# A 128-byte copy per DMA engine as ScalarE's first act, in a rotary-embedding kernel

## Chip, cores, metric

One core of a Trainium2 chip. The metric is device time in microseconds (us); medians are of three to eleven runs, and come with their range or with the ratio to the kernel before and its 95% interval.

## The reference

```python
batch, seq, dim = 16, 512, 1024      # 16 heads of 64, float32
x1, x2 = x[..., :32], x[..., 32:]    # per head
out = concat([x1 * cos - x2 * sin, x1 * sin + x2 * cos], axis=-1)
```

`cos` and `sin` are 512 x 32 and are shared by all batches and heads. `x` and `out` have 33.55 MB each.

## The kernel before

Each of the 16 batches is one tile of 128 partitions x 16 KB (2048 KB). SyncE issues all loads, ScalarE all stores; ten tiles fit into SBUF, so loads 10 to 15 wait for the store of the tile ten before. Between load and store GpSimd and VectorE multiply, and VectorE or TensorE with ScalarE add.

```python
def on_sync(sp):
    for c in range(NC):                               # 16 tiles
        if c * R >= RING:                             # from the 11th: buffer must be free
            sp.wait_ge(sem_out[c - RING // R], 16)
        sp.dma_start(tile(c), xv[c]).then_inc(sem_in[c], 16)
        if c == 0:
            ...                                       # cos and sin to SBUF, 64 KB each
    sp.wait_ge(sem_rest, 16 * (NC - len(sem_out)))

def on_scalar(ae):
    ae.wait_ge(sem_sin, 16)
    sv = ...
    ae.activation(s_sb[:, :, 0, :], sv, COPY, scale=-1.0)
    ae.activation(s_sb[:, :, 1, :], sv, COPY).then_inc(sem_s, 1)
    for u in range(NU):                               # 64 units, 4 a tile
        ...                                           # empties PSUM for some of them
        if r == R - 1:
            wait_added(ae, u)
            ae.dma_start(ov[c], tile(c)).then_inc(...)    # store of tile c
```

## Time and profile before

| | before |
|---|---|
| time, median of the 3 runs before the prediction | 161.97 us (161.94 to 162.54) |
| span of the profiled run | 160.5 us |
| DMA engines full | 38 of 40 slices |
| first load issued, first store issued | 0.80 us, 22.09 us |

Three lines of the timeline (start, duration, engine; ACTq and SPq are DMA issues of ScalarE and SyncE):

```profile
0.80 1.28 ACT L135 ACT_TABLE_LOAD   x1 [0.80 <-PEq L268]
0.80 0.37 SPq L124 DMA_DIRECT2D x_sb<-in_x_dram  x1
...
22.09 0.38 ACTq L144 DMA_DIRECT2D out_dram<-x_sb  x1
```

ScalarE and SyncE start together at 0.80 us. ScalarE's queue has nothing to issue before that first store at 22.09 us.

### The profile page before, as it was taken

The page shows a single profiled execution, that of the slowest core. Times are in us where ns is not written, and L with a number is a line of the kernel's source. Part 1 is how long each engine was busy: PE and PEld are TensorE (multiplying, and loading weights), DVE is VectorE, ACT ScalarE, POOL GpSimd, SP SyncE. Part 2 cuts the span into 40 slices and gives each one's busy share as a digit, 9 for nine tenths or more (in the row PEclk, how much of TensorE's full clock was granted, in tenths as well). Part 3 has the DMA queues.
Part 4 walks back from the last instruction along what each step waited for, and adds up shares of the span by engine and source line. Part 5 has one row for each costly group of instructions (what it writes and reads, how often), then busy time and mean ns, then how long its engine had stood idle before and what let it go on. Part 6 is the DMA issues. An engine that isn't in the chain of part 4 may idle for free.

```text
span 160.5 us, 607 instructions
## 1 busy us (share of the span) xinstructions
PE 81.7 (51%) x102; PEld 25.4 (16%) x102; DVE 131.5 (82%) x116; ACT 26.3 (16%) x27; POOL 130.3 (81%) x62
## 2 busy tenths in 40 slices
PE   6004928354833944854573584575485436576000
PEld 1002402110210220211022021122022002112000
DVE  0089299999999879999999699998999799969400
ACT  3010221122022022012202202211211220220200
POOL 1069999999999999999999993998939988498000
PEclk9999996879595558595765555765567795567555
DMA  5999999999999999999999999999999999999996
GB/s 151 404 445 429 433 429 404 412 441 421 433 445 416 441 433 418 441 421 437 431 425 441 421 441 425 433 437 420 441 429 429 433 425 441 429 429 437 421 435 290
DMA packets 4899, 67.27 MB, mean 419 GB/s; under 512 B 544, under 2 KB 800, under 8 KB 800
## 3 DMA queue, kind: packets, MB, share of 16 engines
q1 hardware_dynamic: 2592, 33.69, 49.9%
q10 hardware_dynamic: 2304, 33.56, 48.8%
q14 instruction: 3, 0.02, 0.0%
HBM read 33.69 MB, written 33.55 MB: 419 GB/s over the span
## 4 chain that ended last, share of the span: by engine, by line
DVE 36%; PE 19%; issue 17%; POOL 10%; ACT 5%; DMA 5%; SPq 0%; DVEq 0%; POOLq 0%
PE t_ps L164 19%; DVE x_sb L235 18%; DVE t_ps L224 15%; POOL t_sb L193 10%; ACT x_sb L141 5%; DMA stage<-in_sin_dram 5%; DVE t_sb L215 4%; SPq L127 0%; SPq L124 0%; ACT s_sb L135 0%; ACT s_sb L136 0%; DVEq L234 0%; DVEq L223 0%; POOLq L116 0%; DVEq L221 0%
## 5 line engine op out<-in xcount | busy, mean ns | idle before, releaser
L193 POOL TENSOR_TENSOR t_sb<-x_sb,s_sb 128x1024 f32<-128x1024 f32 x56 | 129.6, 2376 | 17.0 <-DMA x_sb<-in_x_dram 8.9
L164 PE MATMUL t_ps<-t_sb,ident 128*128 128x512 f32 x96 | 78.9, 972 | 65.8 <-DVE t_ps L224 49.8
L224 DVE TENSOR_TENSOR t_ps<-x_sb,tab_ps 128x1024 f32<-128x1024 f32 x64 | 77.1, 1227 | 10.4 <-ACT x_sb L141 8.6
L235 DVE TENSOR_TENSOR x_sb<-t_ps,t_sb 128x1024 f32<-128x1024 f32 x40 | 48.6, 1217 | 0.0
L141 ACT ACTIVATE x_sb<-t_ps 128x1024 f32<-128x1024 f32 x24 | 24.6, 1023 | 115.8 <-PE t_ps L164 100.9
L164 PEld LDWEIGHTS t_ps<-t_sb,ident 128*128 128x128 f32 x96 | 24.7, 281 | 119.4 <-DVE t_ps L224 86.4
L215 DVE TENSOR_TENSOR t_sb<-x_sb,tab_ps 128x1024 f32<-128x1024 f32 x8 | 9.7, 1210 | 0.0
L202 DVE COPY tab_ps<-stage 128x128 f32<-128x128 f32 x1 | 0.3, 294 | 7.6 <-DMA stage<-in_cos_dram 7.6
L150 PE MATMUL t_ps<-zero 128*128 128x512 bf16 x6 | 2.7, 630 | 1.3 <-DVE zero L198 1.3
L135 ACT ACTIVATE s_sb<-stage 128x128 f32<-128x128 f32 x1 | 0.3, 309 | 6.9 <-DMA stage<-in_sin_dram 6.9
L135 ACT ACT_TABLE_LOAD x1 | 1.3, 1283 | 0.8 <-PEq L268 0.8
L150 PEld LDWEIGHTS t_ps<-zero 128*128 128x128 bf16 x6 | 0.7, 137 | 2.4 <-DVE zero L198 1.2
L198 DVE MEMSET zero<- 128x256 uint32 x1 | 0.3, 272 | 0.9 <-PEq L268 0.9
L175 POOL MEMSET ident<- 128x128 f32 x1 | 0.2, 204 | 0.3 <-POOLq L268 0.3
L177 POOL TENSOR_SCALAR_AFFINE_SELECT ident<-ident 128x128 f32<-128x128 f32 x1 | 0.3, 292 | 0.1
L268 POOL MEMSET const-float32-0.0<- 128x1 f32 x1 | 0.1, 98 | 0.3 <-issue 0.3
L136 ACT ACTIVATE s_sb<-stage 128x128 f32<-128x128 f32 x1 | 0.3, 293 | 0.0
L204 DVE TENSOR_SCALAR tab_ps<-stage 128x128 f32<-128x128 f32 x1 | 0.3, 283 | 0.0
L205 DVE COPY tab_ps<-stage 128x128 f32<-128x128 f32 x1 | 0.3, 283 | 0.0
L268 POOL MEMSET const-bfloat16-1.0<- 128x1 bf16 x1 | 0.1, 101 | 0.0
L268 POOL MEMSET const-uint8-127<- 128x1 uint8 x1 | 0.1, 101 | 0.0
L268 POOL MEMSET const-float32-1.0<- 128x1 f32 x1 | 0.1, 98 | 0.0
## 6 DMA issues: line engine op xcount, KB each, us to landing
x_sb<-in_x_dram SPq DMA_DIRECT2D x16, 2048.0 KB, 52.5
out_dram<-x_sb ACTq DMA_DIRECT2D x16, 2048.0 KB, 19.3
stage<-in_cos_dram SPq DMA_DIRECT2D x1, 64.0 KB, 7.5
stage<-in_sin_dram SPq DMA_DIRECT2D x1, 64.0 KB, 7.2
```

Of the source, the lines that this page charges most:

```text
L135: ae.activation(s_sb[:, :, 0, :], sv, COPY, scale=-1.0)
L136: ae.activation(s_sb[:, :, 1, :], sv, COPY).then_inc(sem_s, 1)
L141: ae.activation(xs[:, k, :], t1_ps[:, u % NT1, :], COPY).then_inc(sem_a, 1)
L150: pe.matmul(t1_ps[:, k, b * BANK:(b + 1) * BANK], zero[:, 0:P], zero[:], start=True, stop=True).then_inc(sem_w, 1)
L164: ins = pe.matmul(t1_ps[:, u % NT1, b * BANK:(b + 1) * BANK], ident[:], t2[:, b * BANK:(b + 1) * BANK], start=False, stop=True, skip_group ...
L177: pl.affine_select(out=ident[:], in_=ident[:], compare_op=mybir.AluOpType.is_equal, fill=0.0, base=0, pattern=[[-1, P]], channel_multiplier=1,
L193: pl.tensor_tensor(t2_sb[:, u % NT2, :, :, :], swapped(k), sin_of(s_sb, r), mult).then_inc(sem_p, 1)
L198: ve.memset(zero[:], 0.0).then_inc(sem_z, 1)
L215: ve.tensor_tensor(t2_sb[:, u % NT2, :, :, :], swapped(k), sin_of(s_ps, r), mult).then_inc(sem_d, 1)
L224: ve.tensor_tensor(t1_ps[:, u % NT1, :].rearrange("p (h d) -> p h d", d=HALF), x_sb[:, k, :, :, :].rearrange("p h t d -> p (h t) d"), c_ps ...
L235: ve.tensor_tensor(xs[:, k, :], t1_ps[:, u % NT1, :], t2_sb[:, u % NT2, :, :, :].rearrange("p h t d -> p (h t d)"), add,).then_inc(sem_v, 1)
L268: nc = _bacc.Bacc("TRN2", target_bir_lowering=False, num_devices=1)
```

## The change

Its intent, as I read it, is that every DMA engine makes one small copy as its first act: 128 bytes from HBM to HBM, into a row of `out`. Whatever an engine's first write there costs would then be paid before the first store, which overwrites the row. The store waits for the copy, so the order is safe. In what follows the copy is called the touch.

```diff
+        sem_touch = stack.enter_context(nc.semaphore("touch"))
 ...
         def on_scalar(ae):
+            ae.dma_start(out[0, 0:seq:seq // 16, 0, 0:HALF], cos[0:seq:seq // 16, :]).then_inc(sem_touch, 16)
             ae.wait_ge(sem_sin, 16)
 ...
                 if r == R - 1:
+                    if c == 0:
+                        ae.wait_ge(sem_touch, 16)
                     wait_added(ae, u)
```

## The prediction

> **What bounds the kernel now.** I read the busy shares first, then the DMA row, then the waits of the loading queue, then the first and last microseconds.
>
> ```profile
> span 160.5 us, 607 instructions
> PE 81.7 (51%) x102; PEld 25.4 (16%) x102; DVE 131.5 (82%) x116; ACT 26.3 (16%) x27; POOL 130.3 (81%) x62
> DMA  5999999999999999999999999999999999999996
> GB/s 151 404 445 429 433 429 404 412 441 421 433 445 416 441 433 418 441 421 437 431 425 441 421 441 425 433 437 420 441 429 429 433 425 441 429 429 437 421 435 290
> ...
> q1 hardware_dynamic: 2592, 33.69, 49.9%
> q10 hardware_dynamic: 2304, 33.56, 48.8%
> ...
> HBM read 33.69 MB, written 33.55 MB: 419 GB/s over the span
> ```
>
> No compute engine is above 82%, but the 16 DMA engines are full in 38 of the 40 slices. 67.1 MB must move (16 loads and 16 stores of 2048 KB each), and the flat part of the GB/s row lies near 430. 67.1 MB / 430 GB/s is 156 us of the 160.5. The other 4.5 us are the start, the end and a few slow places. The chain of waits names VectorE and TensorE, but it follows semaphores and cannot see a queue that is never empty. The waits of the loading queue say it plainly:
>
> ```profile
> SPq L124 <- DMA out_dram<-x_sb: 76.1, 6, 29.1
> SPq L130 <- DMA out_dram<-x_sb: 74.0, 1, 74.0
> ```
>
> Six loads wait 76.1 us in total for an earlier store to leave its buffer; then the queue waits 74.0 us for the last stores. So an engine-microsecond of DMA counts wherever it is spent between the first packet and the last, and nothing else does. To see what time the change could touch I cut the span into stretches (columns: stretch, its length, busy time of each compute engine, TensorE clock, DMA share, GB/s):
>
> ```profile
> 0.00:0.50 0.50, 0.00 (x0) 0.00 (x0) 0.00 (x0) 0.00 (x0) 0.20 (x4) 1.00 0.00 0
> 0.50:1.00 0.50, 0.00 (x0) 0.00 (x0) 0.08 (x1) 0.20 (x1) 0.21 (x2) 1.00 0.00 0
> 1.00:1.50 0.50, 0.25 (x1) 0.13 (x2) 0.20 (x1) 0.50 (x1) 0.29 (x2) 1.00 0.00 0
> 1.50:4.00 2.50, 2.50 (x6) 0.60 (x4) 0.00 (x0) 0.58 (x1) 0.00 (x0) 1.00 0.90 242
> 24.00:29.00 5.00, 3.53 (x4) 1.18 (x4) 4.86 (x5) 1.02 (x1) 5.00 (x3) 0.68 1.00 396
> 29.00:34.00 5.00, 3.49 (x4) 1.08 (x4) 4.96 (x5) 0.00 (x0) 5.00 (x3) 0.66 1.00 429
> 150.00:159.00 9.00, 0.00 (x0) 0.00 (x0) 0.38 (x1) 0.00 (x0) 0.00 (x0) 0.50 1.01 431
> ```
>
> Three things to see. No DMA engine works before 1.5 us. In the first 2.5 us of traffic they are 90% busy but move only 242 GB/s: packets are slow there. And between 24 and 29 us, with the engines still full, the rate is 396 instead of 429: that is just after the first store, which the timeline has at 22.09. Against 429 GB/s the start is short of (429 - 242) x 2.5 us = 468 KB, or 1.1 us; the first store's stretch is short of (429 - 396) x 5 us = 165 KB, or 0.38 us. The queue table agrees in size: q1 (loads) takes 1.1% of 160.5 us = 1.8 us more than q10 (stores) for the same 33.55 MB of x; at 49.9% for 33.69 MB the two tables' 0.13 MB explain 0.3 us, and about 1.4 us is left as slow load packets.
>
> **What the Trainium skill says.** "DMA: Bandwidth & Descriptors", section "Why a DMA increments its semaphore by 16 and not by 1": a DMA runs on the largest number of engines up to 16 that divides its slowest dimension. The touch has 16 rows, so each engine gets one row of 32 floats. No row of this profile has such a transfer; the changed one will. The same page, "Issuing engines are not separate DMA queues": transfers issued from the scalar and sync engines run on the same 16 DMA engines and interleave. The trace agrees: q1 and q10 share the 16 engines at 49.9% and 48.8%. The same page, "Latency and other measured facts": even a tiny transfer needs about 800 ns for an HBM round trip; section "Specifications" adds that below 512 B the engine reads, modifies and writes. This trace has no transfer between two HBM tensors to check either; the 64 KB table loads landed in 7.5 and 7.2 us, but behind 2 MB of x.
>
> **The change part by part.** It removes nothing. It adds one DMA on the scalar queue as that engine's first act, and one wait before the first store.
>
> The wait: the touch goes out at about 0.8 us, the store at 22.1. It would have to take 21 us to hold anything. Cost 0.
>
> The issue: the store issues on this queue take 0.34 us each. The activation table load (1.28 us, from 0.80) shifts to about 1.14 and ends near 2.4; ScalarE then waits for sin until 8.95 us anyway. Cost 0 for compute. If the two issuing engines disturb each other, the first load's issue (0.37 us, also from 0.80) is late by at most 0.34 us; I put 0.1.
>
> The bytes: 16 x 128 B = 2 KB against 67.1 MB; at the rate of the run that is 5 ns. Nothing.
>
> The engines' time at the head: touch and first load are released at the same moment (both 0.80), so the touch does not fall into the idle 1.5 us; it meets the first load at each engine. There each of 16 engines has one extra packet that must read HBM and write HBM. If an engine did nothing else for that round trip it would cost the skill's 0.8 us. But the first load packets are waiting on their own first access in just this stretch (the 1.1 us of shortfall), and a touch that overlaps with that, or pays part of it for the load behind it, costs less. I put 0.3 us, a judgement between 0 and 0.8.
>
> The store's first access: the change's hope must be that each engine's first write to out is expensive and can be paid early. All there is to win in that place is 0.38 us, and part of this stretch may simply be loads and stores beginning to alternate, which a touch does not cure. I put half, -0.2 us.
>
> Sum: 0.1 + 0.3 - 0.2 = +0.2 us, so 161.97 becomes about 162.1 to 162.2.
>
> A late start of compute does not enter. The last store is issued at 150.47; from then to the end the row shows 431 GB/s until 159 and a remnant, 3.8 MB in all, of which the last store is 2.1 MB. So 1.7 MB of older stores, 3.9 us of traffic, still lie ahead of it: compute may slip by almost 4 us before the DMA engines run dry.
>
> **The rivals.** (1) The touch opens the write path in full and for free: 161.97 - 0.38 = 161.6. For it: the dip sits exactly at the first store. Against it: the engines are busy or about to be when the touch arrives, so the cost is moved within the bound, not taken out of it. (2) The touch sits serially at the head of every engine, and its write is slower than a minimal round trip: +0.8 to +1.3 us, 162.8 to 163.3. For it: packets of the first 2.5 us are visibly slow. Against: it is one packet per engine, and engines serve two queues. (3) First access is paid once per engine for reads and writes alike: then the touch pays what the first load paid, the loads behind it run at full rate, and the net is 0 with the dip at 24 us unchanged or shallower: 161.6 to 162.0. (4) The tables land later and everything computes later: +0 by the slack of 3.9 us, unless the delay passes that; nothing suggests it.
>
> **Range and chances.** The sum is +0.2; the largest gain in sight is 0.4 us (0.25%), the largest loss in sight about 1.3 us (0.8%); the three runs of before spread over 0.6 us. 2% is 3.2 us, which no term reaches. Range 161.5 to 162.9. Chances: faster by over 2% 0.01, within 2% 0.97, slower by over 2% 0.02.
>
> **What the changed profile would show.** Right: 16 packets of 128 B more on q10 before 4 us; the stretch from 1.5 to 4 us at or below 242 GB/s; the stretch from 24 to 29 us between 396 and 429; the DMA row still full from the second slice on; the last store issued within a microsecond of 150.5. Wrong in size: a start that is short by more than 1 us over before (rival 2), or no shortfall at all after the first store (rival 1). Wrong altogether: a DMA row with gaps, or a first store much later than 23 us because the touch had not landed.

## The result

161.94 us (161.72 to 162.06, six runs) against 161.95 us (161.85 to 162.54, six runs). The ratio is 0.9992, with a 95% interval of 0.9975 to 1.0008. Ratios here are the mean time of one kernel's fast runs over that of the other's of the same rounds, so not quite the ratio of the medians.

The page after the change:

```profile
span 160.6 us, 608 instructions
...
DMA  4999999999999999999999999999999999999996
GB/s 131 404 457 420 441 432 412 432 420 441 416 445 437 416 441 414 445 428 428 435 420 445 424 428 437 424 437 428 428 437 428 432 432 420 445 428 428 437 416 279
...
q1 hardware_dynamic: 2592, 33.69, 49.6%
q10 hardware_dynamic: 2336, 33.56, 48.9%
...
out_dram<-in_cos_dram ACTq DMA_DIRECT2D x1, 2.0 KB, 6.5
```

The DMA row is as full as before. q1 is the loading queue, q10 ScalarE's storing queue. q10 has 32 packets more: 16 of data and 16 semaphore updates. The last line is the touch: 2 KB, landed 6.5 us after its issue. The loading queue's waits are also the same two:

```profile
SPq L131 <- DMA out_dram<-x_sb: 75.5, 1, 75.5
SPq L125 <- DMA out_dram<-x_sb: 74.7, 6, 27.3
```

The timeline of the start shows the issues. The touch takes 0.63 us to issue, the first load beside it 0.37 us, exactly as before; the activation table moves from 0.80 to 1.46 us, and nobody waits for it.

```profile
0.80 0.63 ACTq L135 DMA_DIRECT2D out_dram<-in_cos_dram  x1
0.80 0.37 SPq L125 DMA_DIRECT2D x_sb<-in_x_dram  x1
...
1.46 1.28 ACT L138 ACT_TABLE_LOAD   x1 [1.46 <-PEq L273]
...
21.79 0.36 ACTq L149 DMA_DIRECT2D out_dram<-x_sb  x1
```

The last line is the first store: the touch had landed at 0.80 + 6.5 = 7.3 us, so its wait held nothing.

And the stretches, with the columns of the prediction:

```profile
1.50:4.00 2.50, 2.49 (x6) 0.60 (x4) 0.00 (x0) 1.24 (x1) 0.00 (x0) 1.00 0.73 210
...
24.00:29.00 5.00, 3.78 (x4) 1.17 (x4) 4.78 (x6) 1.02 (x1) 5.00 (x3) 0.50 0.99 410
29.00:34.00 5.00, 3.44 (x4) 1.17 (x4) 4.97 (x5) 0.00 (x0) 5.00 (x3) 0.50 1.04 446
150.00:159.00 9.00, 2.50 (x4) 0.66 (x2) 3.53 (x4) 1.02 (x1) 0.00 (x0) 0.69 1.01 429
```

On one pair of profiles this looks like the change at work: the start is a little poorer (210 GB/s for 242), and the dip after the first store is shallower (410 for 396, then 446 for 429). One could tell a story of a cost moved from 25 us to the start. The repeats below show that it is no more than chance.

When did the touch reach the engines? Two windows of the DMA table, 1.5 to 5.5 us and 5.5 to 7.1 us, columns queue, packets, MB, share of the 16 engines. First window:

```profile
DMA packets 74, 1.21 MB, mean 303 GB/s; under 512 B 0, under 2 KB 0, under 8 KB 0
...
q1 hardware_dynamic: 74, 1.21, 86.1%
```

Second window:

```profile
DMA packets 70, 0.62 MB, mean 390 GB/s; under 512 B 32, under 2 KB 32, under 8 KB 32
...
q1 hardware_dynamic: 38, 0.62, 91.9%
q10 hardware_dynamic: 32, 0.00, 1.4%
```

No small packet before 5.5 us, all of the touch's after it. In the trace's packet records its data packets start between 5.87 and 6.36 us and last 13 ns each. So the touch is not the engines' first act: it was issued together with the first load and went through behind several of its packets.

### The profile page after: what moved, and what is told of

Its sections match the earlier page's. It is cut to its first block, busy times and chain, and to the rows that moved or that the text cites. A ratio compares the mean times of both kernels' runs of the same rounds, so it can differ in the third digit from the quotient of the medians.

```text
span 160.6 us, 608 instructions
## 1 busy us (share of the span) xinstructions
PE 85.6 (53%) x102; PEld 26.6 (17%) x102; DVE 131.6 (82%) x116; ACT 26.4 (16%) x27; POOL 130.5 (81%) x62
## 4 chain that ended last, share of the span: by engine, by line
DVE 30%; PE 21%; issue 19%; POOL 15%; ACT 5%; DMA 5%; SPq 0%; DVEq 0%; POOLq 0%
PE t_ps L169 21%; DVE x_sb L240 17%; POOL t_sb L198 15%; DVE t_ps L229 10%; ACT x_sb L144 5%; DMA stage<-in_sin_dram 5%; DVE t_sb L220 3%; SPq L128 0%; SPq L125 0%; ACT s_sb L138 0%; ACT s_sb L139 0%; DVEq L228 0%; DVEq L239 0%; POOLq L117 0%
## 5 line engine op out<-in xcount | busy, mean ns | idle before, releaser
L169 PE MATMUL t_ps<-t_sb,ident 128*128 128x512 f32 x96 | 82.8, 1015 | 65.7 <-DVE t_ps L229 52.6
L169 PEld LDWEIGHTS t_ps<-t_sb,ident 128*128 128x128 f32 x96 | 25.8, 295 | 122.2 <-DVE t_ps L229 87.9
```

Source lines behind the costliest of these rows:

```text
L169: ins = pe.matmul(t1_ps[:, u % NT1, b * BANK:(b + 1) * BANK], ident[:], t2[:, b * BANK:(b + 1) * BANK], start=False, stop=True, skip_group ...
```

## The experiments

Fourteen sets of runs were made in all: the two already told and twelve below, of ten different kernels. The theories as they stood at first: WRITE (an engine's first write to `out` is slow, the touch pays it early), RING (the first use of the second queue is slow), CHANCE (the two dips differ as any two executions do), and, for the price, a serial round trip at the head of the queue (rival 2) against the mere time of the issue. The dip is the fall in the rate just after the first store.

### The two kernels again

No edit. Five rounds each, the first two on one chip and the third on another, each beside runs of the kernel before on the same chip.

> The unchanged kernel against itself, for the size of chance. All theories: ratio 1.000 within 0.2%. What I want from it is a second profile: if the first-store dip is a property of the kernel, the stretch from 24 to 29 us again shows about 396 GB/s (before had 396, the changed kernel 410). If the difference of 14 GB/s is chance from one execution to the next (theory CHANCE), this profile shows anything between 390 and 415.

> The changed kernel again. Theory WRITE (each engine's first write to out is slow and the touch pays it early): ratio 0.997 to 1.000, the stretch from 24 to 29 us at 408 GB/s or more. Theory CHANCE: ratio 1.000 within 0.2%, the stretch anywhere between 390 and 415. All: the touch's 16 packets run at 5.8 to 6.4 us, as in the first profile, behind loads that were issued with it.

> The changed kernel a third time. CHANCE: rate from 24 to 34 us between 400 and 428 (so far 428 and 409.5); ratio 1.000 within 0.2%.

Before against itself: ratio 0.9987 (0.9971 to 1.0004), 162.03 us. The changed kernel: 0.9992 (0.9976 to 1.0009), 162.12 us, and the third time 1.0000 (0.9985 to 1.0015), 162.08 us. The kernel before in these two sets: 162.09 and 162.04 us. The first-store stretch of the second profile of the kernel before:

```profile
24.00:29.00 5.00, 3.78 (x4) 1.18 (x4) 4.82 (x5) 1.02 (x1) 5.00 (x3) 0.50 1.02 416
29.00:34.00 5.00, 3.40 (x4) 1.17 (x4) 4.93 (x5) 0.00 (x1) 5.00 (x3) 0.50 1.01 433
```

and of the second profile of the changed kernel:

```profile
24.00:29.00 5.00, 3.53 (x4) 1.17 (x4) 4.86 (x6) 1.02 (x1) 5.00 (x3) 0.67 1.02 396
29.00:34.00 5.00, 3.43 (x4) 1.07 (x4) 4.97 (x5) 0.00 (x0) 5.00 (x3) 0.67 0.99 423
```

The pair has swapped places: now the untouched kernel has 416 and the touched one 396. The third profile of the changed kernel has 383 there. A single profile's dip says nothing about the touch. The start does not either: the untouched kernel's 242 GB/s from 1.5 to 4 us was 223 the second time, the touched kernel's 210 became 223 and 229. The touch's packets started between 5.6 and 6.4 us in both repeats too.

### A touch that writes nothing

```diff
-            ae.dma_start(out[0, 0:seq:seq // 16, 0, 0:HALF], cos[0:seq:seq // 16, :]).then_inc(sem_touch, 16)
+            ae.dma_start(scrap[:], cos[0:seq:seq // 16, :]).then_inc(sem_touch, 16)   # scrap: SBUF
```

> The touch reads the same 16 rows of cos on the same queue but writes to a scratch tile in SBUF, so the queue has been used on every engine and HBM has not been written. WRITE: the stretch from 24 to 29 us is back at about 396 GB/s, as in the kernel before. Theory RING (the first use of the second queue is slow, whatever it carries): 408 or more, as in the changed kernel. CHANCE: no order among the profiles. Time 161.7 to 162.2 us in all.

162.04 us, ratio 0.9993 (0.9973 to 1.0012). The stretch from 24 to 29 us had 413 GB/s. That would have spoken for RING if the repeats had not shown 396 and 383 for kernels that also use the second queue early. Taken with them it is CHANCE. This touch landed in 4.1 us, 2.4 us earlier than the writing one.

### The touch really first

```diff
         def on_sync(sp):
+            sp.dma_start(out[0, 0:seq:seq // 16, 0, 0:HALF], cos[0:seq:seq // 16, :]).then_inc(sem_touch, 16)
...
         def on_scalar(ae):
-            ae.dma_start(out[0, 0:seq:seq // 16, 0, 0:HALF], cos[0:seq:seq // 16, :]).then_inc(sem_touch, 16)
```

> The same touch issued from the loading queue ahead of the first load, so that it really is each engine's first packet. If the head of the queue is serial (my rival 2), every load is later by the touch's round trip: +0.8 us or more, 162.8 us, and the stretch from 1.5 to 4 us falls from 242 to 150 GB/s or lower. If only its issue counts (about 0.4 to 0.6 us on that queue): +0.4 to +0.6, 162.4. If the first access is paid once and the loads behind it then run faster: +0.2 at most. The stretch from 24 to 29 us: WRITE says 408 or more, RING (that queue is the other one) says 396.

162.82 us (162.70 to 163.22), ratio 1.0041 (1.0022 to 1.0060), +0.73 us on the medians. From the timeline of its loading queue:

```profile
0.81 0.61 SPq L122 DMA_DIRECT2D out_dram<-in_cos_dram  x1
1.48 0.56 SPq L126 DMA_DIRECT2D x_sb<-in_x_dram  x1
```

The touch's packets ran from 2.2 to 2.4 us, ahead of all loads, and the first load's issue moved from 0.80 to 1.48 us. That shift, 0.68 us, is about the whole loss; but a round trip of 0.8 us would fit the time as well. The next run tells them apart. The expected "150 or lower" from 1.5 to 4 us came (138), but proves nothing: a later issue alone lowers it. From 24 to 29 us it had 393 GB/s, as RING says; but the changed kernel's repeats, whose second queue was used early, had 396 and 383, so this too is CHANCE.

### No touch, only the later issue

```diff
# the kernel before
         def on_sync(sp):
+            sp.wait_ge(sem_i, 2)
```

> The kernel before, without any touch; the loading queue only waits for GpSimd's identity matrix (done at 1.37 us in the trace of before), so the first load's issue moves from 0.80 to about 1.45 us, as the touch on that queue moved it to 1.48. Theory ISSUE (all of b_sp_first's +0.4% is the later issue of the first load): ratio 1.003 to 1.005, about +0.65 us. Theory ROUND TRIP (the touch's HBM access held the engines in b_sp_first): ratio 1.001 or less here, and b_sp_first's cost is the packets'.

162.72 us, ratio 1.0040 (1.0023 to 1.0058), +0.65 us. The first load of its loading queue:

```profile
1.40 0.36 SPq L125 DMA_DIRECT2D x_sb<-in_x_dram  x1
```

0.60 us later than before costs 0.65 us; 0.68 us later with a touch ahead costs 0.73 us. What a touch costs when it is first is time of issue on the loading queue. A closer look shows all of it. Behind the touch the first load's own issue took 0.56 us instead of 0.37, and in the packet records the first load packet started at 2.69 us instead of 1.80, 0.89 us later, of which 0.68 + 0.19 is issue. From the end of the first load's issue to its first packet there are 0.63 us before, 0.62 here and 0.65 behind the touch: no round trip is added. Rival 2 falls for the round trip and stands for the issue.

### The loads wait for the touch

```diff
# the changed kernel
         def on_sync(sp):
+            sp.wait_ge(sem_touch, 16)
```

> The changed kernel, but the first load waits until the touch has landed: the whole serial price of a touch with nothing ahead of it in the engines. If the 6.5 us from issue to landing in the changed kernel is mostly the queue of load packets ahead of it, the touch lands in 2.5 us or less here, and the time rises by that, to about 164 us. If it is the touch's own latency, it lands after 5 us or more and the time is 167 us or more. If the touch also warms something for the loads, their first packets run at full rate: the first 2.5 us of load traffic then carry well over 242 GB/s.

163.84 us, ratio 1.0108 (1.0092 to 1.0125), +1.77 us. The touch's row in the list of DMA issues (last column: us from issue to landing) and the first load's issue:

```profile
out_dram<-in_cos_dram ACTq DMA_DIRECT2D x1, 2.0 KB, 1.9
```

```profile
2.73 0.37 SPq L126 DMA_DIRECT2D x_sb<-in_x_dram  x1
```

With nothing ahead the touch lands in 1.9 us instead of 6.5: the other 4.6 us come with the loads that were issued beside it. Whether it waited inside each engine or before it, no run here shows. The load goes out 1.93 us later and the kernel ends 1.77 us later. Nor did the loads gain by it: in the 2.5 us of traffic that correspond to 1.5 to 4.0, here 3.43 to 5.93, they moved 229 GB/s, against 223 and 242 in the two profiles of the kernel before. Here a small early copy did not take over the loads' slow first packets.

### More rows

```diff
+            ae.dma_start(
+                out[:, 0:seq:seq // 16, 0, 0:HALF].rearrange("b s d -> s b d"),
+                cos[0:seq:seq // 16, None, :].broadcast_to([16, NC, HALF]),
+            ).then_inc(sem_touch, 16)                  # two_batches: out[0:2, ...] and 2 for NC
```

> The touch copies to 16 rows of each of the 16 batches, 256 rows of 128 B in all, in the same place. If a touched address range is what is warmed (a variant of WRITE), the stores of later batches gain as well: ratio 0.997 or less. CHANCE: 1.000 within 0.3%; the 240 further packets are 15 an engine, at some 13 ns each 0.2 us, so at most +0.2 us. The stretch from 24 to 34 us follows the issue of the first store, not the touch (see the next run).

> e_all_batches once more, to see whether its missing dip comes back. CHANCE: any rate between 400 and 428 from 24 to 34 us. WRITE by range: 424 or more again. Ratio 1.012 to 1.017, as before: 240 more packets of 128 B cost about 2.4 us, 0.16 us each per engine, though their records are 13 ns long.

> The touch copies to 16 rows of batches 0 and 1, 32 rows, two per engine. In e_all_batches the stretch from 24 to 34 us showed 427.5 GB/s, no dip at all, at a price of 2.4 us. If the dip belongs to the address ranges of the first two stores (WRITE by range), it is gone here too, 424 or more, at a price of a fifteenth of 2.4 us = 0.16 us, and the ratio is 0.998 to 1.000. CHANCE: 400 to 428 as in all the others, ratio 0.999 to 1.002.

All batches: 164.54 us, ratio 1.0144 (1.0123 to 1.0166), and again 163.49 us, 1.0098 (1.0073 to 1.0124). Both are slower, by 2.47 and 1.45 us on the medians, the second by less than I had written down. Two batches: 162.11 us, ratio 1.0007 (0.9989 to 1.0026). Stretches of the first profile with all batches:

```profile
4.00:22.00 18.00, 5.42 (x8) 2.23 (x8) 8.17 (x10) 1.53 (x3) 10.21 (x5) 1.00 0.93 391
```

```profile
24.00:34.00 10.00, 3.97 (x6) 1.44 (x7) 9.83 (x9) 1.02 (x1) 10.00 (x5) 0.67 1.00 428
```

of the second:

```profile
24.00:34.00 10.00, 4.88 (x6) 1.61 (x7) 9.83 (x10) 1.02 (x1) 10.00 (x5) 0.78 1.01 431
```

and of two batches:

```profile
24.00:34.00 10.00, 6.63 (x8) 1.78 (x8) 9.83 (x9) 1.02 (x1) 10.00 (x5) 0.68 0.99 408
```

My expectation for the first of these (at most +0.2 us) was wrong: I had priced a row by its 13 ns record. From 4 to 22 us the engines carried 391 GB/s where the kernel before had 429 in the same stretch; (429 - 391) x 18 us is 684 KB, or 1.6 us. Over the 15 further rows of each engine that is about 0.1 us a row, an estimate and an average only. The loss is not spread evenly: from 8 to 9.5 us, where the two tables' 512-byte rows run as well, this kernel moved 81 GB/s and the kernel before 452, and the one further row of the two-batches kernel shows no loss from 4 to 22 us (428 GB/s). What makes that stretch slow is not shown.

In both profiles with all batches the dip after the first store is missing; with two batches it is there. These stretches alone would not show it (428 and 431, against 400 to 428 in all others, and the first store went out at 24.0 and 23.4 us here); the packet records below do. So it can be taken away, but for 1.6 us in place of the 0.4 us or so that it costs. Whether it is the number of early writes, the rows they go to, or the long mixing of reads and writes that takes the dip away, no run here settles. That the first two stores' batches were touched in the two-batches kernel and the dip stayed speaks against "the range must have been touched once".

### Moving the first store

```diff
# the kernel before
                 if r == R - 1:
                     wait_added(ae, u)
+                    if c == 0:
+                        for i in range(8):
+                            ae.activation(scrap[:, i], sv, COPY)      # f_store_late
```

> The kernel before, without a touch; eight small ScalarE copies (about 0.3 us each) hold the first store back, from about 22 to about 24.4 us. In the six profiles so far the mean rate from 24 to 34 us was 424 to 428 GB/s where the first store was issued at 21.6 to 21.8 us (one with the touch, one without, one with the reading touch) and 410 to 415 where it was issued at 22.1 to 22.3 (again with and without). Theory PHASE: the depth of the dip goes with the moment of the store and not with the touch; held back, the dip moves to 26.5 to 32 us and has some depth between 0.15 and 0.5 us of traffic, of which I cannot say which. WRITE: without a touch it stays at about 0.4 us. Time in both: 162.0 within 0.3 us, as the stores have about 4 us of slack at the end.

This experiment failed in its purpose. The store went out at 21.49 us, while six of the eight copies ran from 21.69 us on: the issue did not wait for copies that it does not depend on. It serves as one more profile without a touch: 387 GB/s from 24 to 29 us, 406 from 24 to 34, though issued early. That breaks the PHASE idea (an early first store, at 21.6 to 21.8 us, makes a shallow dip, a later one a deep dip), which had fitted six profiles by luck. Time 162.04 us, ratio 0.9994 (0.9978 to 1.0010).

```diff
# the kernel before
                     wait_added(ae, u)
+                    if c == 0:
+                        ae.wait_ge(sem_v, n_comb[R + 1])              # i_hold_store
```

> f_store_late failed to hold the store (issued at 21.5 us; its copies ran beside the issue). Here the kernel before has its first store wait for VectorE's sum of unit 5, which comes about 3 us later, so the store goes out at 24.5 to 25.5 us. The dip, if it is the store's, moves with it: nothing at 25 to 28, a shortfall at 28 to 33. PHASE as I put it is already broken by f_store_late (issued early, rate 406.5). Its depth: 0.15 to 0.7 us of traffic as in the others. Time 162.0 within 0.4 us; if the 4 us of slack at the end that the prediction worked out are not there, up to +3 us.

Now the store went out at 27.64 us, later than I had expected, and the dip followed:

```profile
27.64 0.38 ACTq L146 DMA_DIRECT2D out_dram<-x_sb  x1
...
24.00:29.00 5.00, 3.78 (x4) 1.18 (x4) 4.73 (x5) 0.93 (x1) 5.00 (x3) 0.50 1.02 436
29.00:34.00 5.00, 3.35 (x4) 1.17 (x4) 4.84 (x5) 0.20 (x2) 5.00 (x3) 0.57 0.99 383
```

So the dip belongs to the first store and not to a time or a load. Its shortfall here is (429 - 383) x 5 us = 230 KB, 0.5 us. The kernel took 162.25 us, ratio 1.0012 (0.9995 to 1.0030): holding the first store back by 5.5 us costs about 0.2 us, and the interval does not exclude 0.

### The dip over all profiles

Mean GB/s from 24 to 34 us, each from that kernel's own profile (the held-back store is left out, as its dip runs over the end of the stretch). A stretch books each 16 KB packet where it starts, and the first store does not come at the same time in all. So the last column is sharper: from the packet records, with each packet's bytes spread over its duration, it is the shortfall against 431 GB/s from 2 us before the first store's first packet to 6 us after it, in us of traffic.

| touch | GB/s | shortfall, us |
|---|---|---|
| none (before twice, f_store_late, c_late_load) | 413, 424, 406, 400 | 0.39, 0.24, 0.50, 0.73 |
| one row an engine (the changed kernel three times, b_sp_first, d_loads_wait) | 428, 410, 403, 415, 411 | 0.19, 0.49, 0.60, 0.48, 0.47 |
| read only | 424 | 0.22 |
| two rows an engine | 408 | 0.48 |
| sixteen rows an engine (two profiles) | 428, 431 | 0.0, 0.0 |

The first two rows lie on top of each other. The last stands apart: in both its profiles every microsecond around the first store moved 431 or 432 GB/s. None of the versions was faster than the two kernels.

## Why the prediction was right

It said 162.1 to 162.2 us, range 161.5 to 162.9, and within 2% with a chance of 0.97; measured 161.94 us. Its steps:

- **The bound.** Right. The DMA row stayed full, and the runs put a number on it: 0.60 us of late first load cost 0.65 us, 1.93 us cost 1.77 us. Time at the head of the queue counts about one for one.
- **The wait costs 0.** Right. The touch landed at 0.80 + 6.5 = 7.3 us, the store went out at 21.79 us.
- **The issue, +0.1.** Too high; it is 0. The touch's issue took 0.63 us, not the 0.34 us of a store, but on a queue that had time; the first load's issue took 0.37 us in both kernels.
- **The bytes, 5 ns.** Nothing in the sum, as said. That a small row can cost far more than its bytes, the all-batches kernel showed: about 0.1 us each on average over 15, though a second row alone showed no cost.
- **The head of the engines, +0.3.** The step's premise failed: the touch does not "meet the first load at each engine". Its packets ran at 5.87 to 6.36 us, behind loads, and not "before 4 us", as the prediction's sign for being right had it. Where it was made to be first, the cost was issue time on the loading queue. In the changed kernel no cost can be seen: 210, 223 and 229 GB/s from 1.5 to 4 us, against 242, 223, 249 and 223 in the four profiles whose first load was issued at 0.80 us without a touch. The means are 221 and 234; (234 - 221) x 2.5 us = 33 KB or 0.08 us, within the scatter. The sign "at or below 242" was therefore empty: the kernel before had 223 itself.
- **The first store, -0.2.** Not there. The dip is real and moves with the first store, but one touch a row deep leaves it where it was: 0.19, 0.49 and 0.60 us by the packet records, against 0.24 to 0.73 without. The sign "between 396 and 429" came in two of three profiles (410, 396, 383). The prediction's reserve, that "a touch does not cure" it, was the better half of that step.
- **The slack of 3.9 us.** It holds. In the changed kernel's first profile the last store went out at 153.6 us, 3 us later than the 150.47 of before; but so it did in the second profile of the kernel before (21.8 to 153.6), and neither ended later. The prediction's sign "within a microsecond of 150.5" was therefore a bad one: the kernel itself does not keep it.

The sum was +0.2 because two costs that do not exist (+0.4) were set against half of a gain that does not exist (-0.2). That these cancelled to within 0.2 us of the truth is luck; that no term could reach 2% is not, and rests on the bound. Of the rivals, the third comes nearest (net 0, dip unchanged), though not for its reason: the loads do not run faster behind a touch.

## What to carry to other kernels

This kernel keeps its DMA engines full from the first packet to the last. Here a warm-up transfer gained nothing in any place it was put, and issued beside the first load it went through behind several of its packets. Before a dip of a few tenths of a microsecond is explained, profile the unchanged kernel twice: here the second took the whole effect away. And measure such a dip packet by packet from the event that it belongs to: fixed stretches blurred it. Do not price a small transfer by its packet record, and put nothing ahead of the first load on the loading queue, where each tenth of issue time came back at the end.

## What the Trainium skill lacked or had wrong

- "DMA: Bandwidth & Descriptors", section "Queues, rings and completion order": it says that an engine drains a whole packet, typically 9 to 17 descriptors, from one queue before it turns to the next. The order of the queues itself no run here shows. The page does not say in time how far behind already queued work a new transfer starts. Here a touch issued with the first load started some 5 us later and landed after 6.5 us, against 1.9 us with nothing ahead; a first store issued at 22.09 us had its first packet in the records at 25.83 us.
- Same page, "Latency and other measured facts": the 800 ns that I took from it as the price of a round trip is a latency, and no engine time. That row of the page does not say so. A touch ahead of the loads cost issue time only (first load packet 0.89 us later, of which 0.68 + 0.19 us is issue; +0.73 us). Alone it landed in 1.9 us, issue included, for a read from HBM and a write to it.
- Same page, "Specifications": its line on transfers below 512 B gives no price, and no page gives one for such rows beside full loads. For rows of 128 B from HBM to HBM the shortfall was 1.6 us for 15 further rows an engine, about 0.1 us a row on average, while the records show 11 to 13 ns; for one further row none was seen.
- No page speaks of the fall in rate when stores first join a stream of loads: 0.19 to 0.73 us of traffic in twelve of these fourteen profiles, at the first store wherever that was put (issued at 27.64 us in the kernel that held it back), and none in the two in which 256 rows of `out` had been written before.
